# Decoder trunk on one core: SBUF tiles moved to multiples of 512 bytes, the output's pieces taken crosswise, the first activations on another DMA queue, and fewer row sums in one attention branch

## The chip, the cores and the metric

The kernel runs on one core of a Trainium2 chip. The metric is device time in microseconds (us) of one execution; lower is better.

## The reference

One layer of a decoder with 256 tokens and a width of 1,024. One projection of the layer's input x feeds five branches of width 384: block attention (A), a mixture of three dilated windows (B), forgetting attention (C), a gated delta rule (D) and cross-attention to a memory (E). Each is gated, projected to 1,024, weighted by a sigmoid and added; an output projection, a residual and a layer norm follow. Cut to what matters here:

```python
h = x @ w_in + b_in                              # 256 x 1024 by 1024 x D_IN, float32
...
# branch B: three (window, dilation) groups g, merged by their softmax denominators
m_max = max over g of row max(logits_g)
num = sum over g of exp(logits_g - m_max) @ v
den = sum over g of rowsum(exp(logits_g - m_max))
o_b = num / den
...
o = o * silu(z)
y = einsum('bsnc,ncd->bsnd', o, w_branch)
y = sum(sigmoid(merge_logits) * y, axis=2)
y = y @ w_out
return layer_norm(DEEPNORM_ALPHA * x + y, ln_g, ln_b)
```

## The kernel before

**Weights in units.** Nearly all the work is 256 tokens times a stream of weight blocks. A `Unit` (L163) is one block of up to 128 x 1,024 float32. `load` (L171) fetches it into one of five `raw` buffers by a DMA on SyncE's queue; `split` (L178) makes two parts of it: ScalarE copies it to `hi` in a shorter float format (L123), and VectorE takes `raw - hi` as `lo` (L124). There are four `hi` and four `lo` buffers. x is split in the same way into `xhi` and `xlo`, once, at the start. A product is then three matmuls (`mm3`, L126): hi by hi, hi by lo, lo by hi. Four units are loaded ahead and two are split ahead.

A matmul holds 128 x 128 values still (LDWEIGHTS) and streams the other operand past them. In most blocks (`fm_unit`, L192) the weights are held and 256 columns of `xhi` or `xlo` stream; in the token-major blocks (`tm_block`, L213) x is held and 402 or 384 columns of the weights stream. The branches' own tensors lie in `f` tiles (the pool `f3`, 3 KB a partition) and `big` tiles (8 KB).

**Where tiles lie.** Pools take SBUF in the order in which they are opened. `cpool` is first, with constants of all sizes, and xhi and xlo are tiles of it: they begin at bytes 16,512 and 24,704 of each partition, 128 past a multiple of 512. The pools behind it (raw, hi, lo, f, big) begin at 62,144, which is 192 past one, and all their tiles have sizes that are multiples of 512, so all of them start 192 past one.

**The start.** The first block is `wcs`, four units of two times 402 columns. Its loads are written by turns with those of x (`load_x`, L278): x comes in two `raw` tiles of four slices each, and all loads are issued by SyncE. After a few zero matmuls the 48 wcs matmuls follow.

**Order.** The blocks follow each other as in a fixed list (`ORDER`). The attention branches, the delta rule and the constants are generators ("side streams") of which a few are advanced by one step after each chunk of a unit. A scheduler then orders each engine's instructions by a simulated timeline; an instruction marked `keep` keeps its place in the program.

**Branch B.** `attend` works pair by pair of heads (three pairs), with three groups of logits and two heads (`x`) each. L752 adds masks and takes extrema; L768 takes exponentials on ScalarE and, with `accum_out`, their row sums, two instructions for each tile; L771 adds the groups' tiles on VectorE; L775 adds the three groups' sums.

**PSUM.** Three `mm` buffers for the units' results, two `lg` tiles of two banks of 512 columns each, one `av`.

**The output.** `w_out` comes in eight units. The result of token tile t (128 tokens) is made in pieces `PC[t]`: two of 512 columns for t = 0, and 512, 256 and 256 for t = 1. Units 0 to 2 are applied to all pieces as they come; for units 3 to 7 each piece gets its 15 last matmuls at the end (`finish`, L1050), piece by piece. `fin["p"][t][i]` says where piece i of tile t lies:

```python
lgs = [lgps() for _ in range(2)]
fin["p"] = [[lg[:, i] for i in range(2)] for lg in lgs]
fin["p"][1].append(mmps((P, 512)))
```

When a piece is ready, L1071 adds the residual and L1072 takes statistics. `norm(t)` (L1054) then merges them, takes the root on ScalarE (L1058), and scales each half of the row by two VectorE operations (L1062, L1063), with one output DMA for each half (L1064), on SyncE's queue for the left and ScalarE's for the right.

Of the kernel before, what the change touches and what calls it, by code (L numbers as in the profile page):

```python
# [9 lines left out]
F32 = mybir.dt.float32  # L10
F32R = mybir.dt.float32r
AF = mybir.ActivationFunctionType
ALU = mybir.AluOpType
# [62 lines left out]
@with_exitstack  # L76
def kernel(ctx: ExitStack, tc: tile.TileContext, T: dict, out: bass.AP):
    nc = tc.nc
    cpool = ctx.enter_context(tc.tile_pool(name="cpool", bufs=1))
    wpool = ctx.enter_context(tc.tile_pool(name="wpool", bufs=3))  # L80
    f3 = ctx.enter_context(tc.tile_pool(name="f3", bufs=16))
    big = ctx.enter_context(tc.tile_pool(name="big", bufs=2))
    sp = ctx.enter_context(tc.tile_pool(name="sp", bufs=4))
    ps = ctx.enter_context(tc.tile_pool(name="ps", bufs=2, space=bass.MemoryType.PSUM))
    dr = ctx.enter_context(tc.tile_pool(name="dr", bufs=1, space=bass.MemoryType.DRAM))
# [6 lines left out]
    def nm(s):  # L92
        uid[0] += 1
        return f"{s}_{uid[0]}"

    def bigt(shape, dt=F32):
        return big.tile(shape, dt, tag="big", name=nm("big"))
# [7 lines left out]
    def ct(name, shape, dt=F32):  # L105
        return cpool.tile(list(shape), dt, name=name)
# [7 lines left out]
    def lgps():  # L114

        return pst("lg", (P, 2, 512), 2)
# [2 lines left out]
        return pst("av", shape, 1)  # L119


    def split(hi, lo, src):
        A_.activation(hi, src, AF.Copy)  # L123
        V_.tensor_tensor(lo, src, hi.bitcast(F32), op=ALU.subtract)  # L124

    def mm3(pt, lh, ll, rh, rl, first, last, pin=False):  # L126
# [10 lines left out]
    HR = (slice(0, 64), slice(64, 128))  # L137


    xhi, xlo = ct("xhi", (P, KD, S), F32R), ct("xlo", (P, KD, S), F32R)  # L140
    cst = ct("cst", (P, C_N))
    vb, vcb = ct("vb", (P, 2, BW)), ct("vcb", (P, BW + 18))
    bcol = ct("bcol", (P, T["bcol"].shape[1]))
# [19 lines left out]
    class Unit:  # L163
# [7 lines left out]
        def load(self):  # L171
            self.r = wpool.tile([P, 1024], F32, tag="raw", name=nm("raw"), bufs=NRAW)
            for i, p in enumerate(self.parts):
                if self.before is not None:
                    self.before[0](i, len(self.parts))
                nc.sync.dma_start(self.r[:, p], self.src[:, p])

        def split(self):  # L178
            self.h = wpool.tile([P, 1024], F32R, tag="hi", name=nm("hi"), bufs=NHI)
            self.l = wpool.tile([P, 1024], F32R, tag="lo", name=nm("lo"), bufs=NHI)  # L180
            for i, p in enumerate(self.parts):
                if self.before is not None:
                    self.before[1](i, len(self.parts))
                split(self.h[:, p], self.l[:, p], self.r[:, p])

    def need(name):
        while name is not None and name not in done:
# [88 lines left out]
    xraw = {}  # L276

    def load_x(i, j, n):  # L278
        if i % 2 == 0 and j == 0:
            xraw["t"] = wpool.tile([P, 4, S], F32, tag="raw", name=nm("raw"), bufs=NRAW)  # L280
        w = 2 // n
        o = 2 * i + w * j
        xraw[i, j] = xraw["t"][:, o % 4:o % 4 + w]
        nc.sync.dma_start(xraw[i, j], T["xT"][:, o:o + w])

    def split_x(i, j, n):
        w = 2 // n
        o = 2 * i + w * j
        split(xhi[:, o:o + w], xlo[:, o:o + w], xraw[i, j])

    def evac_c(p, t):
        if t == 0:
# [10 lines left out]
    def consts():  # L303
        for _ in range(CW):
            yield 1
        nc.sync.dma_start(vcb, T["vcb"].to_broadcast([P, BW + 18]))
        nc.sync.dma_start(bcol, T["bcol"])
        nc.sync.dma_start(cw, T["convw"])
        nc.sync.dma_start(adt, T["adt"].to_broadcast([P, 12]))
        nc.sync.dma_start(cst[:, :C_MA], T["cst"][:, :C_MA])  # L310
        flag("consts")


# [6 lines left out]
    def scalars():  # L320

        yield from wait("sc")
        nc.sync.dma_start(cst[:, C_MA:], T["cst"][:, C_MA:])
        nc.sync.dma_start(gnw, T["gnw"])
        nc.sync.dma_start(mgb, T["mgb"])
        nc.sync.dma_start(vb, T["vb"].to_broadcast([P, 2, BW]))

        V_.tensor_scalar(cwh, cw, 0.5, None, op0=ALU.mult)
        hb = bcol[:, 3 * len(FM):]
# [394 lines left out]
    def attend(br, groups, vname, maskf, width):  # L724
# [5 lines left out]
        def pair(m):  # L730
# [33 lines left out]
            for g in range(ng):  # L764
                for x in range(2):
                    l = L[x][g]
                    for t, sl in SL:
                        A_.activation(l[:, sl], l[:, sl], AF.Exp, bias=mms[x][:, t:t + 1], scale=-1.0, accum_out=sm_[x][:, t, g:g + 1])  # L768
                    yield
                    if g:  # L770
                        V_.tensor_tensor(L[x][0], L[x][0], l, op=ALU.add)  # L771
            for x in range(2):
                rs = spt("rs", (P, 2), bufs=4)
                if ng > 1:
                    V_.tensor_reduce(rs, sm_[x], axis=AX.X, op=ALU.add)  # L775
                    V_.reciprocal(rs, rs)
                else:
                    V_.reciprocal(rs, sm_[x][:, :, 0])
                l = L[x][0]
                for t, sl in SL:  # L780
                    V_.tensor_scalar(l[:, sl], l[:, sl], rs[:, t:t + 1], None, op0=ALU.mult)
# [237 lines left out]
    def out_units():  # L1019
# [12 lines left out]

        def chunk(u, k, t):
            if k == 0 and t == 0:
                lgs = [lgps() for _ in range(2)]
                fin["p"] = [[lg[:, i] for i in range(2)] for lg in lgs]
                fin["p"][1].append(mmps((P, 512)))
                warm = spt("warm", (P, 1), bufs=1)
                A_.activation(warm, yhl[2][0][:, 1, 0:1].bitcast(F32), AF.Sqrt, scale=0.0, bias=0.0)
            if k < 3:  # L1040
                for i in range(len(PC[t])):
                    out_mm(u, k, t, i, k == 0, False)
            elif t == 0:
                late.append((u, k))
# [5 lines left out]
        def finish():  # L1050
            xres, lngb = R["xres"], R["lngb"]
            st2 = [ct(f"st{t}", (P, len(PC[t]), 6)) for t in range(2)]

            def norm(t):  # L1054
                V_.bn_aggr(mv[:, t], st2[t].rearrange("p c s -> p (c s)"))
                rs = rstd[:, t:t + 1]
                V_.tensor_scalar(rs, mv[:, t, 1:2], LN_EPS, None, op0=ALU.add)
                A_.activation(rs, rs, AF.Sqrt)  # L1058
                V_.reciprocal(rs, rs)
                for c, cs in enumerate((slice(0, 512), slice(512, 1024))):  # L1060
                    o = xres[:, t, cs]
                    V_.scalar_tensor_tensor(o, o, mv[:, t, 0:1], lngb[:, 0, cs], op0=ALU.subtract, op1=ALU.mult)  # L1062
                    V_.scalar_tensor_tensor(o, o, rs, lngb[:, 1, cs], op0=ALU.mult, op1=ALU.add)  # L1063
                    (nc.sync, nc.scalar)[c].dma_start(out[t * P:(t + 1) * P, cs], o)  # L1064

            for t in range(2):
                for i, (lo, hi) in enumerate(PC[t]):
                    for x, (u, k) in enumerate(late):
                        out_mm(u, k, t, i, False, x == len(late) - 1)
                    o = xres[:, t, lo:hi]  # L1070
                    V_.scalar_tensor_tensor(o, fin["p"][t][i][:, :hi - lo], 0.5, o, op0=ALU.mult, op1=ALU.add)  # L1071
                    V_.bn_stats(st2[t][:, i], o)  # L1072
                norm(t)
# [139 lines left out]
```

## Time and profile before

| | |
|---|---|
| time, median of 3 runs | 469.86 us (468.28 to 470.16) |
| the profiled execution: its own time | 469.32 us |
| its span | 467.2 us |
| TensorE matmuls in flight | 449.9 us, 96% |
| VectorE busy | 328.1 us, 70% |
| ScalarE busy | 265.5 us, 57% |
| GpSimd busy | 30.6 us, 7% |
| mean granted TensorE clock | 0.994 |
| read from HBM | 79.37 MB |

The span is that of the profiled execution, from its first to its last recorded instruction; its own time is 2.1 us longer. Matmuls are pipelined, so that one is in flight for about 280 ns while the next begins some 115 ns after it: the busy time says that the engine was not idle, not how fast it went.

### The profile page before, as it was taken

The numbers are of one execution on the slowest core, as the hardware profiler recorded it, in microseconds if no ns is written. First come the engines' busy times: TensorE is split into PE (matmuls) and PEld (weight loads), VectorE is DVE, ScalarE is ACT, GpSimd is POOL, SyncE is SP. The second block draws the span as 40 slices with busy tenths as digits, with TensorE's granted clock in tenths as the row PEclk, the third lists the DMA queues.
The fourth block names the chain that finished last, engine by engine and source line by source line (L and its number), as shares of the span: only waits on it lengthen the run. The fifth ranks groups of instructions, "written<-read, shape, count | busy, mean of one in ns | idle before, by whom it ended". The sixth has DMA issues, their size and how long they took to land. (4 is left out here: it accounts for less than half of the span.)

```text
span 467.2 us, 10262 instructions
## 1 busy us (share of the span) xinstructions
PE 449.9 (96%) x4039; PEld 425.0 (91%) x4039; DVE 328.1 (70%) x757; ACT 265.5 (57%) x520; POOL 30.6 (7%) x36
## 2 busy tenths in 40 slices
PE   6999999999999999999999989999989999999993
PEld 3999999999998999999999989988989999999963
DVE  4799998877797535564655689895676565587746
ACT  5466685765666644444434976694684654475600
POOL 0000020010000000000000112100022112200000
PEclk9899999999999999999999999999999999999999
DMA  7978577555445545566434165564765445678202
GB/s 253 380 246 255 164 225 252 159 178 173 125 130 160 152 125 172 176 202 183 125 109 126 60 176 182 173 193 152 250 201 184 145 150 148 190 234 278 91 0 90
DMA packets 35051, 81.38 MB, mean 174 GB/s; under 512 B 8970, under 2 KB 17468, under 8 KB 34876
## 3 DMA queue, kind: packets, MB, share of 16 engines
q1 hardware_dynamic: 34715, 80.22, 55.8%
q8 instruction: 31, 0.51, 0.4%
q10 hardware_dynamic: 288, 0.52, 0.3%
q14 instruction: 17, 0.13, 0.1%
HBM read 79.37 MB, written 1.36 MB: 173 GB/s over the span
## 5 line engine op out<-in xcount | busy, mean ns | idle before, releaser
L124 DVE TENSOR_TENSOR lo<-raw,hi 128x1024 fp32r<-128x1024 f32 (+4 forms) x163 | 169.3, 1040 | 83.4 <-ACT hi L123 80.8
L128 PE MATMUL mm<-xhi,hi 128*128 128x256 f32 x776 | 219.5, 283 | 1.2 <-DVE yt L993 1.2
L128 PE MATMUL mm<-xhi,lo 128*128 128x256 f32 x776 | 216.1, 279 | 1.3 <-DVE lo L124 1.3
L128 PE MATMUL mm<-xlo,hi 128*128 128x256 f32 x776 | 216.5, 279 | 0.0
L123 ACT ACTIVATE hi<-raw 128x1024 fp32r<-128x1024 f32 (+4 forms) x163 | 146.0, 899 | 111.9 <-PE mm L128 83.5
L128 PEld LDWEIGHTS mm<-xhi,hi 128*128 128x128 f32 x776 | 146.3, 189 | 5.8 <-issue 2.7
L128 PEld LDWEIGHTS mm<-xhi,lo 128*128 128x128 f32 x776 | 145.8, 188 | 1.8 <-DVE lo L124 1.7
L128 PEld LDWEIGHTS mm<-xlo,hi 128*128 128x128 f32 x776 | 146.0, 188 | 0.8 <-issue 0.8
L128 PE MATMUL mm<-f,hi 128*128 128x256 f32 x240 | 44.7, 282 | 0.7 <-ACT th L976 0.7
L994 POOL TENSOR_TENSOR yacc<-yacc,yt 128x256 f32<-128x256 f32 x24 | 24.4, 1018 | 280.0 <-DVE yt L993 275.2
L128 PEld LDWEIGHTS mm<-f,hi 128*128 128x128 f32 x240 | 36.6, 188 | 1.6 <-ACT th L976 1.3
L128 PE MATMUL mm<-f,lo 128*128 128x256 f32 x120 | 33.7, 281 | 0.0
L128 PEld LDWEIGHTS mm<-f,lo 128*128 128x128 f32 x120 | 22.6, 188 | 0.0
L128 PE MATMUL mm<-hi,xhi 128*128 128x384 f32 (+1 forms) x48 | 16.6, 363 | 2.1 <-ACT hi L123 2.1
L135 PE MATMUL lg<-f,f 64*128 64x256 f32 (+2 forms) x192 | 18.5, 354 | 0.0
L976 ACT ACTIVATE th<-mm,bcol 128x256 f32<-128x256 f32 x40 | 18.5, 462 | 0.0
L768 ACT ACTIVATE pr<-pr,mm 128x128 f32<-128x128 f32 (+1 forms) x36 | 15.9, 443 | 4.5 <-DVE mm L759 4.5
L128 PE MATMUL mm<-lo,xhi 128*128 128x384 f32 (+1 forms) x48 | 17.3, 360 | 0.4 <-DVE lo L124 0.4
L128 PE MATMUL mm<-hi,xlo 128*128 128x384 f32 (+1 forms) x48 | 17.0, 354 | 0.0
L123 ACT ACTIVATE f<-og 128x256 fp32r<-128x256 f32 x12 | 4.9, 416 | 19.3 <-DVE og L695 15.3
L705 ACT ACTIVATE f<-mm,bcol 128x256 f32<-128x256 f32 x33 | 15.1, 456 | 0.0
L135 PEld LDWEIGHTS lg<-f,f 64*128 64x128 f32 (+1 forms) x192 | 12.5, 186 | 2.6 <-issue 0.9
(221 smaller groups left out, 529.9 us busy)
## 6 DMA issues: line engine op xcount, KB each, us to landing
raw<-in_wf_dram SPq DMA_DIRECT2D x60, 512.0 KB, 4.3
raw<-in_wm_dram SPq DMA_DIRECT2D x40, 512.0 KB, 4.0
raw<-in_wb_dram SPq DMA_DIRECT2D x40, 192.0 KB, 2.5
raw<-in_wt_dram SPq DMA_DIRECT2D x12, 384.0 KB, 3.5
raw<-in_wo_dram SPq DMA_DIRECT2D x8, 512.0 KB, 4.1
gr<-gscr SPq DMA_DIRECT2D x12, 128.0 KB, 3.5
raw<-in_wcs_dram SPq DMA_DIRECT2D x3, 402.0 KB, 5.6
raw<-in_mem_dram SPq DMA_DIRECT2D x2, 512.0 KB, 4.8
```

Of the source, the lines that this page charges most:

```text
L123: A_.activation(hi, src, AF.Copy)
L124: V_.tensor_tensor(lo, src, hi.bitcast(F32), op=ALU.subtract)
L128: ins = PE.matmul(pt, l, r, start=start, stop=stop)
L135: keep(PE.matmul(pt, l, r, start=start, stop=stop))
L705: A_.activation(R[name][:, m], p, AF.Identity, bias=b, scale=1.0 if scale is None else scale)
L768: A_.activation(l[:, sl], l[:, sl], AF.Exp, bias=mms[x][:, t:t + 1], scale=-1.0, accum_out=sm_[x][:, t, g:g + 1])
L976: A_.activation(th, p, AF.Tanh, bias=bcol[:, i:i + 1], scale=0.5)
L994: (V_ if last else G_).tensor_tensor(yacc[:, d], yacc[:, d], yt, op=ALU.add)
```

## The change

**Tile starts.** `xhi` and `xlo` go to a pool of their own that is opened ahead of the others, behind a tile of 96 float32 that nobody reads (`pad`), and `cpool` is opened after `big`. xhi, xlo, raw, hi, lo, f and big then all start at multiples of 512 bytes.

**Start.** x goes to a `big` tile in place of two `raw` tiles. Its first two slices are issued by ScalarE's queue. The instructions of the start, and the loads of the constants, are marked `keep`.

**Branch B.** The exponentials take no sums. The second group is added to the first on GpSimd, and the third on VectorE by an instruction that adds and sums in one; the small sums of three go.

**Output.** The pieces go to the `lg` tiles crosswise, and the right half of token tile 0 is scaled by ScalarE and GpSimd.

```diff
-    cpool = ctx.enter_context(tc.tile_pool(name="cpool", bufs=1))
+    pad = ctx.enter_context(tc.tile_pool(name="pad", bufs=1))
+    xpool = ctx.enter_context(tc.tile_pool(name="xpool", bufs=1))
     wpool = ctx.enter_context(tc.tile_pool(name="wpool", bufs=3))
     f3 = ctx.enter_context(tc.tile_pool(name="f3", bufs=16))
     big = ctx.enter_context(tc.tile_pool(name="big", bufs=2))
+    cpool = ctx.enter_context(tc.tile_pool(name="cpool", bufs=1))
...
-    xhi, xlo = ct("xhi", (P, KD, S), F32R), ct("xlo", (P, KD, S), F32R)
+    pad.tile([P, 96], F32, name="pad")
+    xhi, xlo = [xpool.tile([P, KD, S], F32R, name=n) for n in ("xhi", "xlo")]
...
     def load_x(i, j, n):
-        if i % 2 == 0 and j == 0:
-            xraw["t"] = wpool.tile([P, 4, S], F32, tag="raw", name=nm("raw"), bufs=NRAW)
+        if i == 0 and j == 0:
+            xraw["t"] = bigt([P, KD, S])
         w = 2 // n
         o = 2 * i + w * j
-        xraw[i, j] = xraw["t"][:, o % 4:o % 4 + w]
-        nc.sync.dma_start(xraw[i, j], T["xT"][:, o:o + w])
+        xraw[i, j] = xraw["t"][:, o:o + w]
+        keep((nc.scalar if i == 0 else nc.sync).dma_start(xraw[i, j], T["xT"][:, o:o + w]))
...
-                        A_.activation(l[:, sl], l[:, sl], AF.Exp, bias=mms[x][:, t:t + 1], scale=-1.0, accum_out=sm_[x][:, t, g:g + 1])
+                        A_.activation(l[:, sl], l[:, sl], AF.Exp, bias=mms[x][:, t:t + 1], scale=-1.0,
+                                      accum_out=sm_[x][:, t, 0:1] if ng == 1 else None)
                     yield
-                    if g:
-                        V_.tensor_tensor(L[x][0], L[x][0], l, op=ALU.add)
+
+                    if 0 < g < ng - 1:
+                        G_.tensor_tensor(L[x][0], L[x][0], l, op=ALU.add)
+                    elif g:
+                        for t, sl in SL:
+                            V_.tensor_tensor_reduce(l[:, sl], L[x][0][:, sl], l[:, sl], 1.0, 0.0, ALU.add, ALU.add, sm_[x][:, t, 0:1])
+                        L[x][0] = l
             for x in range(2):
                 rs = spt("rs", (P, 2), bufs=4)
-                if ng > 1:
-                    V_.tensor_reduce(rs, sm_[x], axis=AX.X, op=ALU.add)
-                    V_.reciprocal(rs, rs)
-                else:
-                    V_.reciprocal(rs, sm_[x][:, :, 0])
+                V_.reciprocal(rs, sm_[x][:, :, 0])
...
                 lgs = [lgps() for _ in range(2)]
-                fin["p"] = [[lg[:, i] for i in range(2)] for lg in lgs]
+                fin["p"] = [[lg[:, t_] for lg in lgs] for t_ in range(2)]
                 fin["p"][1].append(mmps((P, 512)))
...
                 for c, cs in enumerate((slice(0, 512), slice(512, 1024))):
                     o = xres[:, t, cs]
+                    if t == 0 and c == 1:
+
+                        nmr = ct("nmr", (P, 1))
+                        V_.tensor_scalar(nmr, rs, mv[:, t, 0:1], -1.0, op0=ALU.mult, op1=ALU.mult)
+                        A_.activation(o, o, AF.Identity, scale=rs, bias=nmr)
+                        G_.tensor_tensor(o, o, lngb[:, 0, cs], op=ALU.mult)
+                        G_.tensor_tensor(o, o, lngb[:, 1, cs], op=ALU.add)
+                        nc.scalar.dma_start(out[t * P:(t + 1) * P, cs], o)
+                        continue
```

How the instructions stand, at three places. First SyncE's DMAs at the start of the program, before (`raw` and `big` tiles carry a number; `in_xT` is x, `in_wcs` the first weights, `in_wf` the weights after them):

```order
L284 DMA raw_105<-in_xT_dram 128x256
L176 DMA raw_104<-in_wcs_dram 128x402
L284 DMA raw_105<-in_xT_dram 128x256
L176 DMA raw_104<-in_wcs_dram 128x402
L284 DMA raw_105<-in_xT_dram 128x512
L176 DMA raw_110<-in_wcs_dram 128x804
L284 DMA raw_114<-in_xT_dram 128x512
L176 DMA raw_113<-in_wcs_dram 128x804
L284 DMA raw_114<-in_xT_dram 128x512
L306 DMA vcb<-in_vcb_dram 128x402
L176 DMA raw_117<-in_wcs_dram 128x804
```

and after, where the first two loads of x stand on ScalarE's queue, ahead of its first activation:

```order
L183 DMA raw_111<-in_wcs_dram 128x402 x2
L293 DMA big_112<-in_xT_dram 128x512
L183 DMA raw_117<-in_wcs_dram 128x804
L293 DMA big_112<-in_xT_dram 128x512
L183 DMA raw_120<-in_wcs_dram 128x804
L293 DMA big_112<-in_xT_dram 128x512
L183 DMA raw_123<-in_wcs_dram 128x804
L183 DMA raw_126<-in_wf_dram 128x1024
L183 DMA raw_168<-in_wf_dram 128x1024
L183 DMA raw_188<-in_wf_dram 128x1024
L183 DMA raw_206<-in_wf_dram 128x1024
L315 DMA vcb<-in_vcb_dram 128x402
```

The second wcs unit moves from the sixth place to the fourth, x holds no `raw` buffer any more, and vcb, the constants that the wcs results wait for, moves from ahead of the fourth wcs unit to behind four wf units.

Second, TensorE at the border of token tile 0's two pieces in `finish`, before (`lg_6041` is a PSUM tile, `hi`/`lo`/`f` streamed and `f` held):

```order
L128 MATMUL lg_6041<-hi_6101,f_1005_5801 128x512
L128 MATMUL lg_6041<-lo_6102,f_1005_5801 128x512
L128 MATMUL lg_6041<-hi_6101,f_1006_5802 128x512
L128 MATMUL lg_6041<-f_993_5744,f_1043_5977 128x512
L128 MATMUL lg_6041<-f_995_5746,f_1043_5977 128x512
```

and after:

```order
L134 MATMUL lg_6047<-hi_6107,f_1004_5807 128x512
L134 MATMUL lg_6047<-lo_6108,f_1004_5807 128x512
L134 MATMUL lg_6047<-hi_6107,f_1005_5808 128x512
L134 MATMUL lg_6048<-f_992_5750,f_1042_5983 128x512
L134 MATMUL lg_6048<-f_994_5752,f_1042_5983 128x512
```

The matmuls stand in the same order; the second piece (the fourth row on) now goes to the other `lg` tile.

Third, ScalarE's last instructions, before (`rstd` is the root of `norm`, `big_4561` holds residual and result):

```order
L123 ACTIVATE hi_6101<-raw_6061 128x1024
L1058 ACTIVATE rstd<-rstd 128x1
L1064 DMA out_dram<-big_4561 128x512
L1058 ACTIVATE rstd<-rstd 128x1
L1064 DMA out_dram<-big_4561 128x512
```

and after:

```order
L127 ACTIVATE hi_6107<-raw_6067 128x1024
L1070 ACTIVATE rstd<-rstd 128x1
L1078 ACTIVATE big_4567<-big_4567,nmr,rstd 128x512
L1081 DMA out_dram<-big_4567 128x512
L1070 ACTIVATE rstd<-rstd 128x1
L1085 DMA out_dram<-big_4567 128x512
```

Between the two roots there is now an activation over 512 columns, and the DMA behind it sends what GpSimd has made of its result.

## Rows read from the trace of the kernel before

**Rows 1.** The page: busy time of each engine, share of the span, instructions.
```profile
span 467.2 us, 10262 instructions
PE 449.9 (96%) x4039; PEld 425.0 (91%) x4039; DVE 328.1 (70%) x757; ACT 265.5 (57%) x520; POOL 30.6 (7%) x36
```

**Rows 2.** Waits of PE, longest sums: us in total, times, longest us.
```profile
PE mm L128 <- ACT hi L123: 2.1, 3, 1.4
...
PE lg L128 <- DVE big L1071: 1.6, 2, 0.8
```

**Rows 3.** Windows (us): busy PE, PEld, DVE, ACT, POOL, granted clock, DMA share, GB/s.
```profile
10.00:20.00 10.00, 9.60 (x48) 9.23 (x47) 7.82 (x27) 4.95 (x8) 0.00 (x0) 0.83 1.04 377
20.00:50.00 30.00, 30.00 (x263) 29.72 (x262) 28.85 (x79) 19.14 (x30) 0.00 (x0) 1.00 0.81 261
```

**Rows 4.** The chain that ended last, its end: start us, us, what.
```profile
389.80 45.80 PE mm L128 x396
...
443.93 3.44 PE lg L128 x15
...
447.40 0.70 DVE big L1071
...
448.14 7.15 PE lg L128 x30
...
456.06 2.06 PE lg L128 x15
```

**Rows 5.** The timeline of the start: start us, us, engine, line, operation; wait in brackets.
```profile
1.64 0.42 SPq L284 DMA_DIRECT2D raw<-in_xT_dram  x1
...
7.32 0.33 SPq L176 DMA_DIRECT2D raw<-in_wcs_dram  x1
...
9.70 0.45 PE L128 MATMUL mm<-hi,xhi 128*128 128x402 f32 x1 [1.37 <-ACT hi L123]
...
17.13 0.34 PE L128 MATMUL mm<-lo,xhi 128*128 128x402 f32 x1
...
18.41 0.35 PE L128 MATMUL mm<-hi,xlo 128*128 128x402 f32 x1
```

**Rows 6.** The timeline of PE, ends of stretches of one operand: start us, us.
```profile
11.99 0.54 PE L128 MATMUL mm<-hi,xhi 128*128 128x402 f32 x1
...
13.66 0.54 PE L128 MATMUL mm<-hi,xlo 128*128 128x402 f32 x1
...
29.94 0.28 PE L128 MATMUL mm<-xhi,hi 128*128 128x256 f32 x1
...
42.06 0.28 PE L128 MATMUL mm<-xhi,lo 128*128 128x256 f32 x1
...
226.75 0.28 PE L128 MATMUL mm<-xhi,lo 128*128 128x256 f32 x1
...
230.76 0.28 PE L128 MATMUL mm<-xhi,hi 128*128 128x256 f32 x1
...
318.80 0.40 PE L128 MATMUL mm<-big,hi 128*128 128x256 f32 x2
...
320.00 0.28 PE L128 MATMUL mm<-big,hi 128*128 128x256 f32 x1
```

**Rows 7.** Groups of instructions by form: count, busy us, mean ns, idle before.
```profile
L768 ACT ACTIVATION_READ_ACCUMULATOR pr<-pr,mm 128x1 f32 x36 | 6.8, 188 | 0.0
...
L771 DVE TENSOR_TENSOR pr<-pr,pr 128x384 f32<-128x384 f32 x12 | 6.6, 554 | 5.1 <-ACT pr L768 5.0
...
L752 DVE CUSTOM_DVE_ANT_0 pr<-lg,cst 128x256 f32<-128x256 f32 x24 | 10.0, 418 | 0.0
...
L994 POOL TENSOR_TENSOR yacc<-yacc,yt 128x256 f32<-128x256 f32 x24 | 24.4, 1018 | 280.0 <-DVE yt L993 275.2 <-DVE mm L759 4.8
```

**Rows 8.** One line's instructions each: least, median, most ns, from to (us); forms.
```profile
L994 POOL TENSOR_TENSOR yacc<-yacc,yt x24: 741/990/1658, 252.3 to 406.8; 128x256 f32<-128x256 f32 x24
...
L124 DVE TENSOR_TENSOR lo<-raw,hi x163: 499/1218/1767, 4.8 to 442.3; 128x1024 fp32r<-128x1024 f32 x106, 128x384 fp32r<-128x384 f32 x40, 128x768 fp32r<-128x768 f32 x12, 128x804 fp32r<-128x804 f32 x3
```

More of the change, by code (lines that the diff above doesn't have):

```diff
@@ L119, in avps, with split @@
         return pst("av", shape, 1)
-    def split(hi, lo, src):
-        A_.activation(hi, src, AF.Copy)
+    def split(hi, lo, src, pin=False):
+        ins = A_.activation(hi, src, AF.Copy)
+        if pin:
+            keep(ins)
         V_.tensor_tensor(lo, src, hi.bitcast(F32), op=ALU.subtract)
@@ L175, in load @@
                     self.before[0](i, len(self.parts))
-                nc.sync.dma_start(self.r[:, p], self.src[:, p])
+                ins = nc.sync.dma_start(self.r[:, p], self.src[:, p])
+                if self.before is not None:
+                    keep(ins)
         def split(self):
@@ L183, in split @@
                     self.before[1](i, len(self.parts))
-                split(self.h[:, p], self.l[:, p], self.r[:, p])
+                split(self.h[:, p], self.l[:, p], self.r[:, p], self.before is not None)
     def need(name):
@@ L288, in split_x @@
         o = 2 * i + w * j
-        split(xhi[:, o:o + w], xlo[:, o:o + w], xraw[i, j])
+        split(xhi[:, o:o + w], xlo[:, o:o + w], xraw[i, j], True)
     def evac_c(p, t):
@@ L305, in consts @@
             yield 1
[L306 to L310, printed above, removed]
+        keep(nc.sync.dma_start(vcb, T["vcb"].to_broadcast([P, BW + 18])))
+        keep(nc.sync.dma_start(bcol, T["bcol"]))
+        keep(nc.sync.dma_start(cw, T["convw"]))
+        keep(nc.sync.dma_start(adt, T["adt"].to_broadcast([P, 12])))
+        keep(nc.sync.dma_start(cst[:, :C_MA], T["cst"][:, :C_MA]))
         flag("consts")
@@ L322, in scalars @@
         yield from wait("sc")
[L323 to L326, printed above, removed]
+        keep(nc.sync.dma_start(cst[:, C_MA:], T["cst"][:, C_MA:]))
+        keep(nc.sync.dma_start(gnw, T["gnw"]))
+        keep(nc.sync.dma_start(mgb, T["mgb"]))
+        keep(nc.sync.dma_start(vb, T["vb"].to_broadcast([P, 2, BW])))
         V_.tensor_scalar(cwh, cw, 0.5, None, op0=ALU.mult)
```

## The prediction

> **What bounds the kernel now.** The page comes first: of a span of 467.2 us TensorE has matmuls in flight for 449.9, VectorE 328.1, ScalarE 265.5 [rows 1]. Busy time of a pipelined engine does not say that it works at its best rate, so two questions follow: where TensorE does not run, and how fast it goes where it runs. The waits answer the first. Beyond the first 20 us and the last 24, TensorE hardly ever waits; the largest entries are the split of the first weights and VectorE's reads in the output stage [rows 2]. The windows show the rest: from 20 to 50 us TensorE is busy for all of 30 us, but VectorE for 28.85 of them [rows 3]; a faster TensorE would find VectorE close behind it there. The chain that ended last runs through matmuls almost alone until the end, where two reads by VectorE stand in it [rows 4]. So three places can move the end: TensorE's start, its pace, its last 16 us.
>
> **Output pieces crosswise.** Before, both column halves of token tile 0 lie in one PSUM tile, and both `lg` pieces of tile 1 in the other. In the chain the 15 matmuls of the first piece are followed by 0.70 us of VectorE at L1071 and only then by matmuls; before the last piece but one, of 256 columns, the same thing happens [rows 4]. The matmuls of the next piece go to another bank of the same tile, so they need nothing of that read: 447.38 to 448.14 and 455.30 to 456.06, 0.76 us each, are a wait between neighbours in one tile. After the change, neighbours lie in different tiles, as the order shows; a tile comes back one piece later, 3.4 us after its read began. Nothing is late next on TensorE. **1.5 us less on the path**, 0 if the read is waited for in some other way.
>
> The other half of this edit moves one quarter of the final scaling (tile 0, right half) from VectorE to an activation on ScalarE and two multiplies/adds of 512 columns on GpSimd. GpSimd takes 1,018 ns for 256 columns [rows 7], so about 2.0 us each by proportion, an estimate. Tile 0's last matmul then ends near 450.9 (447.4 and another 3.44), its mean and root some 2 us later, so GpSimd starts near 453, with an end near 459. ScalarE's queue issues that output behind it, and behind the issue stands ScalarE's square root for tile 1. The last matmul ends near 458.4 (456.06 and two pieces of 2.0, less the 1.5 of the waits), and that root comes due about 1.3 us after it, at 459.7; its result is wanted only after two more VectorE operations, about 1.3 us later. So the edit is hidden by about a microsecond; were GpSimd as slow as in its longest row (1,658 ns [rows 8], 3.3 us each at 512 columns), about 1.5 us would come back. I take nothing.
>
> **First x on ScalarE's queue, x outside the weight buffers.** Before, SyncE issues x and wcs by turns, and the fourth wcs load is not issued until 7.32, since x holds two of the five weight buffers [rows 5]. TensorE starts wcs unit 1 at 9.70, waiting for ScalarE's split, and the last of the 48 wcs matmuls at 18.41 [rows 5]. After the change SyncE's second wcs unit is its fourth load instead of its sixth, 0.84 us sooner at 0.42 us an issue [rows 5]; the last wcs load goes at about 4.0. Two bounds: if DMA bandwidth does not care (the DMA share is already 1.04 from 10 to 20 us [rows 3]), only the earlier issue counts, 0.8 us. At the other end: the 36 matmuls from 9.70 would take 36 x 0.183 = 6.6 us at the later pace (seven steps from 17.13 to 18.41 [rows 5]), but took 8.9 (9.70 to 18.41 and one step), because the granted clock in 10 to 20 us was 0.83 [rows 3], with the rows from 11.99 to 13.66 at 1.2 GHz [rows 6], after TensorE had idled for 1.37 us before 9.70 [rows 5]. If the gap shrinks enough for the clock to stay up, that gives about 2 us more, 3.0 together. **I take 2.0.** What is late instead are the constants: vcb now stands behind four wf loads, and VectorE adds it behind three wf splits. Adding up bytes in the new order (4.8 MB before vcb, at the 377 GB/s of rows 3, from 2 us on), it lands near 15 us. TensorE then still has its third PSUM buffer, 2.8 us of work, so this costs nothing unless vcb is later than about 18.
>
> **Row sums of branch B.** It drops 36 accumulator reads of 188 ns on ScalarE (6.8 us), twelve 554 ns adds and six small reductions on VectorE, and puts in six pairs of a fused add-and-sum and six GpSimd adds of 384 columns (about 1.5 us by proportion). The nearest row for the fused form is 418 ns for 256 columns [rows 7], by proportion 0.63 us a pair, 3.8 us against the 6.6 of the adds, so VectorE has about 2.9 us less. The work lies at 255 to 345 us, where TensorE waits hardly at all. **Nothing on the path**; TensorE's 449.9 us cover it.
>
> **Multiples of 512 bytes.** Before, xhi and xlo begin 128 bytes past a multiple of 512, and raw, hi, lo, f3 and big 192 past one. All begin on one after it. No row shows a matmul on such a tile, so I read the pace against the start of the tile that streams through (the first name behind the arrow; all have 256 columns, 106.7 ns at 2.4 GHz). From xhi/xlo: 107 steps from 29.94 to 42.06, 113.3 ns; in other stretches 34 steps from 226.75 to 230.76, 117.9. From big (192 past): ten steps from 318.80 to 320.00, 120.0 [rows 6]. At 1.2 GHz 402 columns take 334 ns (five steps, 11.99 to 13.66 [rows 6]), exactly a column a cycle, so what is above 106.7 is an extra that the streaming at full clock shows. The pace is thus worse the further the start lies from a multiple, and 512 is beyond what the trace can tell. Bounds: nothing; and the whole extra. Whole: 396 matmuls took 45.80 us [rows 4], 115.7 each on average, 9.0 above; times the 2,808 matmuls of 256 columns (97 units of 24, 40 of 9, mk's 72, the output's 48) 25.3 us, and 13.3 to 16 ns for the 216 wider ones (15 of 512 columns in 3.44 us [rows 4] are 229 ns against 213.3), 3 us: 28 together. I take the row that lies nearest to a multiple, the best pace of the trace, for all: 2,808 x 2.4 = 6.7, and 216 x 6.7 ns = 1.4. **8.1 us.** VectorE's 96% from 20 to 50 us allows 4% there, more than the 2% this needs.
>
> **Sum.** The profiled execution took 469.32 us, 2.1 beyond its span: 469.3 - 1.5 - 2.0 - 8.1 = 457.7. The median of the runs is 0.54 higher, so 458.3.
>
> **Rivals.**
> *The starts of tiles do nothing.* Then 113 against 117.9 ns for the same tiles (which the trace has) says that something else sets the pace, phases of the pipeline for instance, and big and xhi differ for what precedes them. Against it: each of the two starts keeps to its paces. 469.9 - 3.5 = 466.4. The Trainium skill, SBUF — State Buffer, section "Door 1: The DMA port swizzle", names 16-byte lines as what an access pays for crossing; all the starts here, old and new, are multiples of 16, so by that rule the time would be this rival's. The rows of 113.3 and 120.0 do not bear it out, but they differ in more than the start.
> *Aligned tiles go nearly at a column a cycle.* Halfway, 110 ns, is 2,808 x 5.7 = 16.0 and 216 x 10 = 2.2: 469.9 - 3.5 - 18.2 = 448.2; the whole 28 would be 438. For it: the step from 192 to 128 past already buys 6.7 ns, as much as is left. Against: VectorE at 96% from 20 to 50 us.
> *GpSimd's adds hold up VectorE* (the other side). Place: branch B, 255 to 345 us. VectorE's split of 1,218 ns in the median took 1,767 at worst [rows 8], in stretches where GpSimd had work, so the two can hinder each other. Price: six adds of 1.5 us, 9.2 us, if each stops VectorE in full and TensorE behind it; it decides once TensorE waits for more than 3.5 us and the tiles give nothing: 469.9 - 3.5 + 9.2 = 475.6. Against it: two units are split ahead, 5 us of cover, and VectorE has a third of its time free there. The Trainium skill, SBUF — State Buffer, "Who interferes with whom", says that a VectorE instruction with two SBUF inputs and a GpSimd one that reads SBUF block each other in full; the trace's 0.55 us agrees in kind.
>
> **How the numbers follow.** Chances: the forecast 0.45 (its own range 452 to 463: 0.8 to 3.0 at the start, 3 to 12 from the tiles), no effect of the starts 0.22, nearly a column a cycle 0.23, the whole 28 us 0.05, GpSimd 0.05. To hold 8 in 10 the range must reach both middle rivals: 445 to 467. Half a per cent, 2.3 us, is about what a measurement can tell from no change; 467.5 is that bound. Forecast and both fast cases lie under it; the rival without effect lies 1.1 below, and at 467.6 with only the 0.8 at the start, so I count 0.10 of its 0.22 and 0.02 of the forecast's as no change: faster 0.83, the same 0.12, slower 0.05.
>
> **What would show it.** In the changed kernel's trace: the chain's end with no VectorE piece between the `lg` matmuls; wcs unit 1 starting before 9; steps of 113 ns or less everywhere, big and f tiles included, and none of 118 to 120; POOL's last operation ended before ScalarE's root is due. The prediction is wrong if xhi steps still come at 113 and 118, if TensorE newly waits for VectorE's split or for vcb near 18 us, or if the steps fall to 107 to 110.

## The result, and the profile after

The changed kernel takes 471.54 us (median of 8 runs, 471.21 to 472.63), the kernel before 469.33 us on the same chips (8 runs, 466.79 to 470.54). The ratio is 1.0058, with a 95% interval of 1.0035 to 1.0081: slower by about 2.2 us, where 11 us less were forecast. The two profiled executions, from which the rows before and after come, took 469.32 and 472.48 us: the one after lies 0.9 above its median, and the last section shows where.

The page of the profiled execution after, against [rows 1]:

```profile
span 470.7 us, 10250 instructions
PE 459.5 (98%) x4039; PEld 437.7 (93%) x4039; DVE 325.5 (69%) x762; ACT 263.8 (56%) x485; POOL 40.3 (9%) x44
```

TensorE has the same 4,039 matmuls as before, and matmuls in flight for 9.6 us more. What it waits for (us in total, times, longest) became less, against [rows 2]:

```profile
PE mm L134 <- ACT th L987: 1.4, 1, 1.4
PE lg L327 <- DVE zero L324: 1.2, 1, 1.2
PE mm L134 <- ACT hi L127: 0.9, 1, 0.9
PE mm L134 <- DVE yt L1004: 0.2, 1, 0.2
```

No split on VectorE and no piece of the output is in the list any more; before, beside the output's entry in [rows 2], there was

```profile
PE mm L128 <- DVE lo L124: 1.7, 3, 0.7
```

So TensorE waits less and takes longer: it goes slower. The chain that ended last shows it at one stretch that both kernels have, 396 matmuls of 256 columns in a row near the end (start us, us, what), against the first and the later rows of [rows 4]:

```profile
393.55 47.70 PE mm L134 x396
...
449.59 12.02 PE lg L134 x60
```

Before, the 396 took 45.80 us, 115.7 ns each; now 47.70, 120.5 each. (In both, 288 of the 396 stream xhi or xlo and 108 stream f.) The second row is the other side of the account: the 60 last matmuls into the `lg` tiles (15 more into an `mm` tile follow) run through in 12.02 us with no read by VectorE among them, where before three stretches (3.44, 7.15 and 2.06) and two waits of 0.76 made 14.2.

The windows answer to [rows 3] (busy PE, PEld, DVE, ACT, POOL, granted clock, DMA share, GB/s):

```profile
10.00:20.00 10.00, 10.00 (x67) 10.00 (x67) 8.93 (x31) 6.89 (x10) 0.00 (x0) 1.00 1.00 379
20.00:50.00 30.00, 30.00 (x252) 30.00 (x251) 27.09 (x74) 17.23 (x28) 0.00 (x0) 1.00 0.76 259
```

In the first 10 us stretch the granted clock is 1.00 in place of 0.83, and the window holds 67 matmuls in place of 48. From 20 to 50 us it is the other way: 252 in place of 263, at the same granted clock, and with VectorE less busy than before (27.09 against 28.85). VectorE does not hold TensorE there.

Set against each other, matmul by matmul (the 3,072 that `mm3` issues, counted from 0 in their order; the two orders differ in a few short stretches, none of them at the numbers below), the two traces give this account; negative is ahead of before:

| at the start of | before, us | after, us | difference |
|---|---|---|---|
| the first matmul that streams xhi (number 48) | 18.60 | 15.93 | -2.7 |
| number 888 | 136.87 | 137.29 | +0.4 |
| number 1,728 | 259.99 | 263.33 | +3.3 |
| number 2,208 | 337.78 | 338.42 | +0.6 |
| number 2,928 | 432.67 | 438.21 | +5.5 |
| the last | 459.64 | 463.13 | +3.5 |

The start gains 2.7, the long stretches on either side of branch B lose 6.0 and 4.9, the stretch with branch B gains 2.7, the output gains 2.0.

### The profile page after: what moved, and what is told of

Same layout as the page of the kernel before. It is cut to its first block, busy times and chain, and to the rows that moved or that the text cites. A ratio compares the mean times of both kernels' runs of the same rounds, so it can differ in the third digit from the quotient of the medians.

```text
span 470.7 us, 10250 instructions
## 1 busy us (share of the span) xinstructions
PE 459.5 (98%) x4039; PEld 437.7 (93%) x4039; DVE 325.5 (69%) x762; ACT 263.8 (56%) x485; POOL 40.3 (9%) x44
## 4 chain that ended last, share of the span: by engine, by line
PE 96%; DVE 1%; DMA 1%; ACT 1%; issue 0%; POOL 0%; DVEq 0%; ACTq 0%
PE mm L134 79%; PE lg L141 4%; PE lg L134 4%; PE av L141 2%; PE lg L798 1%; DMA big<-in_xT_dram 1%; PE lg L651 1%; DVE pr L785 0%; PE lg L941 0%; PE lg L873 0%; PE lg L645 0%; PE lg L448 0%; ACT pr L777 0%; PE lg L667 0%; DVE big L1083 0%
## 5 line engine op out<-in xcount | busy, mean ns | idle before, releaser
L130 DVE TENSOR_TENSOR lo<-raw,hi 128x1024 fp32r<-128x1024 f32 (+4 forms) x163 | 167.6, 1029 | 93.1 <-ACT hi L127 92.8
L134 PE MATMUL mm<-xhi,hi 128*128 128x256 f32 x776 | 224.0, 289 | 0.2 <-DVE yt L1004 0.2
L134 PE MATMUL mm<-xlo,hi 128*128 128x256 f32 x776 | 221.2, 285 | 0.0
L134 PE MATMUL mm<-xhi,lo 128*128 128x256 f32 x776 | 220.7, 284 | 0.0
L134 PEld LDWEIGHTS mm<-xhi,hi 128*128 128x128 f32 x776 | 149.2, 192 | 5.3 <-issue 3.4
L134 PEld LDWEIGHTS mm<-xlo,hi 128*128 128x128 f32 x776 | 149.4, 192 | 0.8 <-issue 0.8
L134 PEld LDWEIGHTS mm<-xhi,lo 128*128 128x128 f32 x776 | 149.3, 192 | 0.0
L761 DVE CUSTOM_DVE_ANT_0 pr<-lg,cst 128x128 f32<-128x128 f32 (+1 forms) x48 | 14.1, 350 | 1.1 <-PE lg L141 1.1
```

The costliest lines, as they stand in the source:

```text
L134: ins = PE.matmul(pt, l, r, start=start, stop=stop)
L761: V_.tensor_tensor_reduce(l[:, sl], pts[x][:, sl], mk[x][:, sl], 1.0, 3.0e38, ALU.add, ALU.min, mx[x][:, t, g:g + 1])
```

## The experiments

Two theories stood at the outset. **Relative:** a weight load runs while the matmul ahead of it streams (from 20 to 50 us after, both are busy for all of 30.00 us), so two reads of one engine lie side by side, and what counts is the difference between the starts of the held and the streamed tile. Before, the weights lay 64 bytes past x (192 against 128); after, the difference is 0; f and big always had 0, and big was slow before, too (120.0 [rows 6]). **Absolute:** the start of the streamed tile counts by itself, and 128 past a multiple of 512 is better than 0. The rival to both: the layout does nothing, and the pace is a mode that an engine keeps when it is never interrupted.

The pace is told by the row of the chain for the same 396 matmuls. Where an experiment changes the layout alone, every engine's instructions stand in the same order as in the kernel that it was made from.

### The layout alone, and everything but the layout

```diff
 # e1, the kernel before
-    cpool = ctx.enter_context(tc.tile_pool(name="cpool", bufs=1))
+    pad = ctx.enter_context(tc.tile_pool(name="pad", bufs=1))
+    xpool = ctx.enter_context(tc.tile_pool(name="xpool", bufs=1))
...
-    xhi, xlo = ct("xhi", (P, KD, S), F32R), ct("xlo", (P, KD, S), F32R)
+    pad.tile([P, 96], F32, name="pad")
+    xhi, xlo = [xpool.tile([P, KD, S], F32R, name=n) for n in ("xhi", "xlo")]
```

(with `cpool` behind `big`; the second kernel takes the same lines out of the changed one.)

> The kernel before with the layout alone: xhi, xlo, raw, hi, lo, f and big all start at multiples of 512, and every engine's instructions stand as before. If the starts of tiles set the pace (whether the two operands' starts against each other, or each by itself), the matmuls of 256 columns from xhi and xlo follow each other at 120 ns, as in the changed kernel, not at 113 to 118: 2,231 of them by about 5 ns, 8 to 11 us, so about 478 to 480. If the pace comes from the other edits (a TensorE that is never interrupted), the steps are as before and the time is 469 within 1.

> The changed kernel with the pools in the old order: xhi and xlo again 128 past a multiple of 512, the weights and f and big 224 past one. If the starts set the pace, steps from xhi fall back to 113 to 116 ns and the time to about 462 to 464 (471.5 less about 8). If the other edits do, steps stay at 120 and the time at 471.

Measured: the layout alone 478.26 us, ratio 1.0191 (1.0154 to 1.0227), 9 us slower than the kernel before; everything but the layout 467.93, ratio 0.9981 (0.9959 to 1.0003). The chains' rows, of the layout alone:

```profile
396.30 47.70 PE mm L130 x396
```

and without the layout:

```profile
389.33 47.24 PE mm L132 x396
```

The first is the pace of the changed kernel to the hundredth, in a program in which nothing else changed. The rival is out: the layout does it. The second missed its number: 119.3 ns, not 113 to 116. What is different in that kernel, and stood in the expectation without being used: with one small constant more in `cpool`, the weights lie at 224, not 192, so the difference to x is 96 and not 64. That was a first hint that the difference counts, and which one; the kernel of matmuls alone, below, shows 117.4 at 96 and 113.8 at 64. So this run does not tell what everything but the layout is worth; the next pair does.

### The same difference elsewhere, another difference at the same place

```diff
 # e3: all tiles 128 past a multiple of 512
-    pad.tile([P, 96], F32, name="pad")
+    pad.tile([P, 128], F32, name="pad")
 # e4: x at 0, all pools behind it 64 past
+    pad2 = ctx.enter_context(tc.tile_pool(name="pad2", bufs=1))
     wpool = ctx.enter_context(tc.tile_pool(name="wpool", bufs=3))
...
+    pad2.tile([P, 16], F32, name="pad2")
```

> The changed kernel with 128 bytes more in front of all these tiles: all of them start 128 past a multiple of 512, streamed and held operand alike. If what counts is how the two operands' starts lie to each other, nothing changes: steps of 120 ns, 471.5. If the start of the streamed tile counts by itself (128 past is where xhi lay before), steps of 113 to 116, about 463.

> The changed kernel with 64 bytes between xlo and the pools behind it: xhi and xlo start at a multiple of 512, weights, f and big 64 past one. If the starts to each other count, steps from xhi and xlo go at 113 to 116 ns, those from f and big (64 past, as their weights) at 120, and the time is about 463. If the start of the streamed tile counts by itself, xhi stays at 120 and the time at 471; if any start that is no multiple of 512 is good, f and big go faster too.

Measured: all at 128, 471.47 us, ratio 1.0047 (1.0030 to 1.0064); the weights 64 past x, 462.48 us, ratio 0.9857 (0.9817 to 0.9897). The chain with all at 128:

```profile
392.25 47.70 PE mm L134 x396
```

and with the weights 64 past x:

```profile
384.24 45.80 PE mm L135 x396
```

Moving everything changes nothing; moving the weights by 64 bytes against x, which stays at a multiple of 512, gives back the pace of before to the hundredth. The absolute theory is out: one difference at two pairs of places (0 and 0, 128 and 128) gives 47.70 twice, another (128 and 192 before, 0 and 64 here) gives 45.80 twice. f, which lay at 64 as its weights did, stayed at 118 to 119 ns in the mean. This kernel also has the differences of before together with all the other edits; it takes 6.7 us less than the kernel before (469.18 beside it), so that is what the other edits are worth together.

### Other differences

The same edit with other paddings, x at 0 always, and a second padding behind the weights, which gives f and big a difference of their own:

> The changed kernel with the weights starting 32 bytes past x, and f and big 64 before the weights (all modulo 512). So far the held operand's start less the streamed one's has given these steps: 0: 120 ns; 64: 113 to 118, 115 in the mean; 96: 118. If the pace depends on that difference and any difference but 0 helps, x's steps go below 120, and f and big (64, which had 0) go to 113 to 118; the time is between 458 and 465. If only 64 is good, x's steps stay near 120 and the time is 469 to 471.

> The changed kernel with the weights 128 bytes past x, and f and big 32 before the weights. If the difference counts in a period of 128 bytes, x's steps are 120 ns again, and the time 469 to 471. If it counts in a longer one, 128 is at least as good as 64: 113 to 115 ns, 462 or less. f and big show the difference of 32 beside the run that has it for x.

> The changed kernel with the weights 64 bytes before x (448 past it), and f and big 96 before the weights. With a period of 128 the difference of 448 is that of 64: x's steps 113 to 118 ns and the time about 463. If the sign counts, and the weights must lie behind the streamed tile, steps are nearer 120 and the time 467 or more.

> The changed kernel with the weights 256 bytes past x, and f and big 128 before the weights. With a period of 128, 120 ns everywhere and 469 to 471. With a period of 512, this is the furthest apart that they can be, and 113 ns or less everywhere: 460 or less.

| weights less x, bytes | 396 matmuls, us | ns each | time, us | ratio (95%) |
|---|---|---|---|---|
| 0 (changed kernel) | 47.70 | 120.5 | 471.54 | 1.0058 (1.0035 to 1.0081) |
| 32 | 46.84 | 118.3 | 466.69 | 0.9964 (0.9945 to 0.9982) |
| 64 | 45.80 | 115.7 | 462.48 | 0.9857 (0.9817 to 0.9897) |
| 128 | 47.16 | 119.1 | 468.99 | 0.9998 (0.9977 to 1.0020) |
| 256 | 47.56 | 120.1 | 471.19 | 1.0058 (1.0038 to 1.0078) |
| 448 | 46.84 | 118.3 | 466.69 | 0.9967 (0.9948 to 0.9986) |

108 of the 396 stream f; the steps of the other 288 are 120.0, 118.1, 114.1, 118.8, 119.7 and 117.8 ns in the mean, from the top. Against the expectations: 32 helped, but not down to 465 us; 128 and 256 came near what a period of 128 asks for (469 to 471 us), and 448 did not (about 463). No simple period came out. A period of 128 would have made 128 equal to 0 and 448 equal to 64; it did neither. 256 is as 0, so it is no period of 512 with its best in the middle, either. What holds is that 64 is the best of the six, and 0 and 256 the worst. In the first of these kernels f and big, with a difference of 64, showed big's steps at 114.5 ns in place of 119.6.

### The two reads by themselves

This kernel leaves out all but matmuls: it has no weights from memory and no other engine at work while it measures. It ran once. The streamed tiles are cut from one padded tile at 20 offsets:

```diff
+    def group(o, i):
+        x = [t[:, o:o + KD * S].rearrange("p (k c) -> p k c", k=KD) for t in (xh, xl)]
+        for k in range(KD):
+            for j, (a, b) in enumerate(((0, 0), (0, 1), (1, 0))):
+                keep(nc.tensor.matmul(pt[i], w[a][:, k], x[b][:, k], start=k == 0 and j == 0, stop=k == KD - 1 and j == 2))
```

> Leaves out the whole computation: only matmuls of 256 columns, three for each of eight slices as in a unit, on constant data, no DMA and no other engine beside them, 48 for each of 20 differences between the held and the streamed operand's start (0 to 112 in steps of 16, 128 to 480 in steps of 32), once upwards and once downwards. If the two reads of one engine get into each other's way, the pace varies with the difference here too: 120 ns at 0 and 256, lowest near 64, between them elsewhere, and the same upwards and downwards. If other engines' and DMA traffic is needed for it, all 20 go at one pace, 107 to 113 ns.

Each block's time is that from its first matmul's start to the next block's, divided by 48, in ns:

| difference | up | down | | difference | up | down |
|---|---|---|---|---|---|---|
| 0 | 120.0 | 119.9 | | 192 | 117.8 | 117.9 |
| 16 | 117.2 | 117.3 | | 224 | 116.7 | 117.9 |
| 32 | 118.3 | 118.3 | | 256 | 120.0 | 119.9 |
| 48 | 119.2 | 119.2 | | 288 | 118.4 | 118.3 |
| 64 | 113.8 | 113.7 | | 320 | 117.9 | 117.8 |
| 80 | 119.2 | 119.2 | | 352 | 118.8 | 118.6 |
| 96 | 117.4 | 117.3 | | 384 | 118.5 | 118.7 |
| 112 | 116.6 | 118.6 | | 416 | 119.9 | 119.9 |
| 128 | 119.9 | 118.7 | | 448 | 113.4 | 113.4 |
| 160 | 119.9 | 119.7 | | 480 | 116.9 | 116.7 |

Five of these blocks, as windows of that kernel's trace (differences 0, 64, 256 and 448 upwards, 448 downwards; a window counts the 48 matmuls that start in it and those in flight at its edges):

```profile
17.04:22.80 5.76, 5.76 (x50) 5.76 (x49) 0.00 (x0) 0.00 (x0) 0.00 (x0) 1.00 0.01 3
39.82:45.29 5.47, 5.47 (x51) 5.47 (x50) 0.00 (x0) 0.00 (x0) 0.00 (x0) 1.00 0.00 0
85.01:90.77 5.76, 5.76 (x51) 5.76 (x50) 0.00 (x0) 0.00 (x0) 0.00 (x0) 1.00 0.00 0
119.25:124.70 5.45, 5.45 (x51) 5.45 (x50) 0.00 (x0) 0.00 (x0) 0.00 (x0) 1.00 0.00 0
135.91:141.35 5.44, 5.44 (x51) 5.44 (x49) 0.00 (x0) 0.00 (x0) 0.00 (x0) 1.00 0.02 3
```

To see here are zeros under VectorE, ScalarE and GpSimd, a granted clock of 1.00, next to no DMA, and yet 5.76 us against 5.45 for the same 48 matmuls. No other engine is needed: the pace comes out of TensorE alone. Only the streamed tile's start changes here, so that it is the difference that counts rests on the two pairs above; what the two reads do to each other inside the engine no trace shows. 0 and 256 are the worst, 64 and 448 (64 the other way) the best, and for most differences both directions agree.

The difference does not settle the pace alone. At 112, 128 and 224 the two directions differ by 1.2 to 1.9 ns, so what ran before has a part there. And in the whole kernel one difference has two paces. Of the blocks of 24 steps from x that run without a pause, 35 of 45 go at 113 to 114 ns in the kernel before and 9 at 118 (the two paces of xhi in [rows 6]); with the weights 64 past x in the changed kernel 29 of 46 and 17; with 448, 1 of 46 and 45 (118 to 119). With 0 all 46 go at 120. The same stretch, from 27 to 47 us, in the kernel before and with the weights 64 past x, both with a difference of 64:

```profile
27.00:47.00 20.00, 20.00 (x179) 20.00 (x178) 20.00 (x54) 12.80 (x20) 0.00 (x0) 1.00 0.79 252
27.00:47.00 20.00, 20.00 (x172) 20.00 (x171) 19.11 (x51) 12.41 (x21) 0.00 (x0) 1.00 0.78 258
```

What picks one of the two stays open, and with it why 448, as good as 64 here, gave 117.8 in the whole kernel.

### f and big, too

```diff
...
+    pad2.tile([P, 16], F32, name="pad2")     # wpool 64 past a multiple of 512
+    pad3.tile([P, 112], F32, name="pad3")    # f3 and big again at one
```

> The weights 64 bytes past x, and f and big back at multiples of 512, so that the weights lie 64 past all that streams against them. The 360 steps from f and 72 from big then go at 115 to 118 ns in place of 118 to 120: 1 to 1.5 us below the run with the weights, f and big all at 64 (462.5), so about 461. If f and big stay at 119, the difference does not count for them.

Measured: 461.33 us, ratio 0.9824 (0.9792 to 0.9856), the fastest of all, 1.8% below the kernel before. Steps from f went from 117.7 and 119.1 (with `hi` and with `lo` held) to 114.7 and 114.6 ns, those from big from 119.8 to 116.9. The chain:

```profile
384.95 45.11 PE mm L136 x396
```

113.9 ns each. The 1.1 us against the kernel with weights, f and big all at 64 are within the intervals; the pace is not in doubt.

### Branch B as before

The changed kernel with L768 to L776 of before:

```diff
-                        A_.activation(l[:, sl], l[:, sl], AF.Exp, bias=mms[x][:, t:t + 1], scale=-1.0,
-                                      accum_out=sm_[x][:, t, 0:1] if ng == 1 else None)
+                        A_.activation(l[:, sl], l[:, sl], AF.Exp, bias=mms[x][:, t:t + 1], scale=-1.0, accum_out=sm_[x][:, t, g:g + 1])
                     yield
-                    if 0 < g < ng - 1:
-                        G_.tensor_tensor(L[x][0], L[x][0], l, op=ALU.add)
...
+                    if g:
+                        V_.tensor_tensor(L[x][0], L[x][0], l, op=ALU.add)
```

> The changed kernel with branch B's sums as before: row sums with each exponential, adds on VectorE. As predicted, the edit lies off the path: 471.5 within 0.7. If it took waits of TensorE away (4.6 us of idle between 260 and 350 us before, 1.7 after), the time is 1.2 to 2.9 us longer: 472.7 to 474.4, and TensorE again waits for VectorE's lo and for ScalarE's f and th there.

Measured: 473.82 us, ratio 1.0102 (1.0075 to 1.0130). TensorE's waits in this kernel from 250 to 350 us:

```profile
PE mm L134 <- DVE lo L130: 0.7, 2, 0.4
PE mm L134 <- ACT f L884: 0.7, 1, 0.7
PE mm L134 <- ACT th L985: 0.6, 1, 0.6
PE mm L134 <- DVE yt L1002: 0.3, 1, 0.3
PE mm L134 <- DVE big L130: 0.2, 1, 0.2
```

The edit lies on the path, then, by waits of TensorE for the splits and for ScalarE that it takes away. How much: 2.3 us by the medians, which the intervals leave open between almost nothing and 4 (every run, 472.87 to 474.76, lies above every run of the changed kernel); 1.5 us by the traces, matmul by matmul against the kernel with all tiles at 128 (0.2 us behind it at number 1,728, 1.7 at the end). Idle time is 0.7 of these 1.5 (2.46 us here between 250 and 350, 1.73 there); the rest is not traced to a cause.

### x as before

```diff
-        if i == 0 and j == 0:
-            xraw["t"] = bigt([P, KD, S])
+        if i % 2 == 0 and j == 0:
+            xraw["t"] = wpool.tile([P, 4, S], F32, tag="raw", name=nm("raw"), bufs=NRAW)
...
-        keep((nc.scalar if i == 0 else nc.sync).dma_start(xraw[i, j], T["xT"][:, o:o + w]))
+        keep(nc.sync.dma_start(xraw[i, j], T["xT"][:, o:o + w]))
```

> The changed kernel with x again in two raw buffers and issued by SyncE, by turns with the weights. The start then is that of before: TensorE waits 1.2 to 1.4 us ahead of the second unit of wcs, the granted clock is 0.83 between 10 and 20 us, and the time is 2.0 to 2.7 us longer, 473.5 to 474.2. If the gain at the start came from the instructions kept in order and not from x, it stays at 471.5.

Measured: 473.89 us, ratio 1.0114 (1.0077 to 1.0152), 2.4 us above the changed kernel. Its window and waits at the start:

```profile
10.00:20.00 10.00, 9.60 (x49) 9.32 (x48) 6.54 (x8) 5.71 (x8) 0.00 (x0) 0.83 0.93 325
```

```profile
PE mm L134 <- ACT hi L127: 2.1, 2, 1.2
PE mm L134 <- DVE lo L130: 0.4, 1, 0.4
```

The wait, the lower clock and the time of the start are back, with the instructions still kept in order: it is x, its queue and its buffers together.

## Why the prediction was wrong

**Multiples of 512 bytes: the step that failed.** The sum took 8.1 us off for them; alone they add 9.1. The rows were read rightly: 113.3 and 117.9 ns from xhi, 120.0 from big [rows 6]. The step from them was "the pace is thus worse the further the start lies from a multiple". It sorted two starts, 128 and 192, by the distance of the streamed tile alone, and went on to a third. The held tile's start stood in the same paragraph (192 for the weights) and was not put beside it. With it, the rows of before allow another reading, which the runs bear out: xhi lies 64 from its weights and is the faster, big and f lie 0 from theirs and are slower, and the change gives every pair a difference of 0. Read so, the forecast would have been 120 ns for all: the 2,328 matmuls from xhi and xlo go from 114.9 to 119.8 ns a step in the mean (steps without a pause), 11.4 us. That one start had two paces, 113.3 and 117.9, was a sign besides that a start by itself does not set the pace. The layout alone measured 9.1, and 8.4 between the two traces: its first xhi matmul came 1.0 us sooner, and TensorE's idle time between 250 and 350 us fell by 1.7. The windows' sums over that stretch, of the kernel before:

```profile
sum 100.00, PE 95.41 PEld 89.86 DVE 77.24 ACT 71.58 POOL 11.62; mean PE 47.70 PEld 44.93 DVE 38.62 ACT 35.79 POOL 5.81
```

and of the layout alone:

```profile
sum 100.00, PE 97.06 PEld 91.56 DVE 74.75 ACT 69.62 POOL 9.61; mean PE 48.53 PEld 45.78 DVE 37.37 ACT 34.81 POOL 4.81
```

4.6 us and 2.9 us without a matmul in flight: a slower TensorE waits less for its helpers.

**The rivals.** "The starts of tiles do nothing" fell with the layout alone. Its page, the Trainium skill, SBUF — State Buffer, section "Door 1: The DMA port swizzle", speaks of 16-byte lines; the pace table has multiples of 16 alone and runs from 113.4 to 120.0, so that rule does not decide here. "Nearly a column a cycle" did not occur: no block of one difference gave less than 113.4 ns. "GpSimd's adds hold up VectorE" did not, either: undoing branch B made the kernel slower. (VectorE had less room than that rival was told: it is busy for 70.83 of the 90 us from 255 to 345, so a fifth is free and not a third.) No rival had the true mechanism, and none on the slow side was about TensorE's own pace.

**Output crosswise: right.** 1.5 us were forecast, 2.0 measured (5.5 behind at number 2,928, 3.5 at the end). Both waits are gone. Each cost more than its 0.76: before, the starts on either side lay 1.17 us apart (446.97 to 448.14, 454.89 to 456.06), 0.94 more than a step of 0.23. GpSimd's part was hidden as forecast; the timeline after has (start us, us):

```profile
460.88 1.29 POOL L1079 TENSOR_TENSOR big<-big,big 128x512 f32<-128x512 f32 x1 [48.76 <-ACT big L1078]
462.24 1.28 POOL L1080 TENSOR_TENSOR big<-big,big 128x512 f32<-128x512 f32 x1
464.82 0.20 ACT L1070 ACTIVATE rstd<-rstd 128x1 f32<-128x1 f32 x1 [4.02 <-DVE rstd L1069]
```

1.29 us each where 2.0 were estimated by proportion, and an end at 463.52; ScalarE's root for tile 1, the last row, begins at 464.82, when its input is ready, 0.9 us after ScalarE has issued that output (463.56, 0.35). That is the forecast's "about a microsecond", with luck: GpSimd began 4.5 us after tile 0's last matmul (456.42), where 2 were taken, and its shorter adds made up for it. This edit was not undone by itself; what it gave is read from the trace.

**First x on ScalarE's queue: right, near its upper bound.** 2.0 forecast, with 0.8 and 3.0 as bounds; 2.4 us by the medians, 2.6 by the traces (against the kernel with all tiles at 128, at the last matmul), undoing it. The second wcs unit starts at 9.06 in place of 9.70, a little later than the sign asked for. The clock staying up is the larger part: from there to the first xhi matmul it takes 6.87 us at 1.00, and 8.94 in the kernel with x as before, at 0.83. The old order does not always bring the lower clock: the layout alone, whose instructions stand as before, has in its profiled execution

```profile
10.00:20.00 10.00, 9.40 (x56) 9.05 (x57) 8.63 (x27) 5.37 (x9) 0.00 (x0) 1.00 0.92 328
```

with 1.00, and that is the 1.0 us by which its trace is ahead there. So part of this gain may differ from one execution to the next. vcb was not late: TensorE waits nowhere for the sums that need it.

**Branch B: wrong in that it was put off the path.** "The work lies at 255 to 345 us, where TensorE waits hardly at all" overlooked that nearly all the waits that TensorE has between the start and the output lie just there: 4.6 us of idle time. Each was short (1.2 us and less), so none stood at the head of the list. It gave about 1.5 to 2.3 us.

**The sum again**, with what was measured: +9.1 for the layout, -2.5 for x, -1.5 to -2.3 for branch B, -2.0 for the output make +2.3 to +3.1, against +2.2. The three edits beside the layout come to -6.0 to -6.8 by these terms, and to -6.7 in one run, the kernel with the weights 64 past x. The forecast had -3.5 for them: they gave nearly twice that, and hid most of what the layout cost.

## What to carry to other kernels

When matmuls with a weight load each go slower than their columns, look at where the held and the streamed tile start against each other, not at either alone; a layout that looks tidy can give both the same start, modulo 512 bytes, which was among the slowest cases here. Here 64 bytes of padding ahead of the weights are worth 9 us of 471. Two starts are not a trend: before a row is extended to a case that the trace does not show, name every other thing that differs between the rows.

## What the runs showed of the hardware that was not expected

- The pace of matmuls of 256 columns with one weight load each depends on the difference of the two starts, in steps as fine as 16 bytes: 120.0 ns at 0, 117.2 at 16, 119.2 at 48, 113.8 at 64, 119.2 at 80, with no engine or DMA beside them. For 384 streamed columns of x's products 64 is no gain (173 to 174 ns in the median at 0 and at 64 either way); with 96 between them they took 175 to 177. For 512 (the output, f held) it is none either: 227 ns at 0, 229 to 231 with the weights 64 past f.
- The same wait need not cost the same. Ahead of 341 us TensorE waits 1.4 us in one piece for ScalarE in the changed kernel and with all tiles at 128 alike. From 340 to 350 us the changed kernel's profiled execution then shows

```profile
340.00:350.00 10.00, 8.73 (x59) 8.53 (x60) 6.87 (x16) 6.79 (x11) 2.09 (x3) 0.83 0.58 189
```

and the one with all tiles at 128

```profile
340.00:350.00 10.00, 8.55 (x69) 8.35 (x70) 7.32 (x16) 6.98 (x11) 2.96 (x3) 1.00 0.62 207
```

A granted clock of 0.83 against 1.00, and 59 matmuls against 69: 1.5 us between two programs whose instructions stand alike, which is about the spread of the changed kernel's own runs (471.21 to 472.63).
